# Modulation of the attention layer from plain 32-bit weights in four column groups of TensorE

## Chip, cores, metric

One NeuronCore of a Trainium2 chip runs the whole kernel in one launch. The metric is device time in microseconds (us), the median of several executions. Engines: TensorE (PE, with its weight loads as PEld), VectorE (DVE), ScalarE (ACT), GpSimd (POOL), and SyncE (SP), which issues most of the DMAs.

## What is computed

Two layers over 1024 latent tokens and 256 context tokens of width 1024: windowed attention with a context prefix, then a Conformer convolution module, each with a residual. Only the start matters here, the modulation of the first layer (i = 0):

```python
silu_c = jax.nn.silu(c)            # c: (1, 1024)
silu_cc = jax.nn.silu(c_ctx)       # c_ctx: (1024,)
shift, scale, gate = jnp.split((silu_c @ ada_w[i] + ada_b[i])[:, None, :], 3, axis=-1)
h_lat = modulate(rmsnorm(x, norm_g[i]), shift, scale)          # h * (1 + scale) + shift
shift_c, scale_c, gate_c = jnp.split(silu_cc @ ada_w[i] + ada_b[i], 3, axis=-1)
h_ctx = modulate(rmsnorm(h_ctx_stream, norm_g[i]), shift_c, scale_c)
proj = h_lat @ w_in                # w_in: 1024 x 5120
```

`ada_w[0]` is 1024 x 3072. Two rows, one for the latent and one for the context vector, are multiplied with its first 2048 columns (shift and scale); the gate columns and the second layer's modulation are computed elsewhere and stay as they are.

## The kernel before

The large products are written as three products of a reduced 32-bit type (`F32R`): each operand is rounded to a high part (on ACT) and the rest is kept as a low part (on DVE or POOL), and high x high, high x low and low x high are summed in PSUM (`mm3`). A plain `F32` product is also possible on TensorE and is used in a few places of the kernel, the means of the layer norm among them.

The modulation of layer 1 is worked in four column pairs, `pr` = 0 to 3. A pair covers 256 shift columns and the 256 scale columns that belong to them, which are what two 128-row tiles `kt` of the transposed, modulated input need. For each pair:

- `ada_load(pr)` issues eight 256 KB DMAs on SP into four pages `araw` (each page holds two 128-row slices of the 1024 rows, 512 columns) and two 1 KB DMAs that put the bias into row 4 of a half page `R[pr]`.
- `ada_split(pr)` rounds each page to a high part `ahi` on ACT and subtracts it on DVE to get the low part `alo`.
- `ada_mm(pr)` multiplies on TensorE. The stationary operand is `c4`, 128 rows by 4 columns per slice: high parts of the two silu vectors, then their low parts. The moving operand is a slice of `ahi` or `alo`, 512 columns. Sixteen matmuls, 128*4 by 128x512, accumulate into 4 rows of one PSUM bank. I call these sixteen matmuls a modulation block. DVE copies the four rows to rows 0 to 3 of `R[pr]`.
- `ada_cols(pr)` turns rows into columns: four plain matmuls of `R[pr][0:5]` with a 5 x 2 selection matrix `sel`, which adds high and low rows and the bias. DVE writes the result to `mod`.
- `x_tile(kt)` then modulates a transposed tile of the normalised x: ACT writes the high part `hh`, DVE the full value `hf`, and DVE or POOL the low part `hl`. `c_tile(kt)` does the same for the context.

Around this, `spin(n)` issues matmuls on zeros ahead of the first real work. The loop over `pr` does `ada_mm(pr + 1)`, then 6 or 9 matmuls of `x_mm` for tile 2 pr, the transposes of the next tile of x, `ada_cols(pr + 1)`, `x_mm` of tile 2 pr + 1, and the next transposes. In the third turn two context tiles are worked between. TensorE keeps the program's order in the whole kernel (`PE.on`); DVE keeps it in the opening (`pin("PV")`), ACT only at its very start (`pin("PVA")`); POOL and SP, and later ACT and DVE, are ordered by a planner with a cost model.

The pages `pg` (45 of 4 KB per partition) and half pages `hp` (6) are handed out in the order in which they were freed.

Of the kernel before, what the change touches and what calls it, by code (L numbers as in the profile page):

```python
# [9 lines left out]
F32 = mybir.dt.float32  # L10
F32R = mybir.dt.float32r
AF = mybir.ActivationFunctionType
ALU = mybir.AluOpType

P = 128
# [3 lines left out]
KT = D // P  # L19
# [13 lines left out]
ADA_FP = ()  # L33
# [61 lines left out]
def backbone_kernel(  # L95
# [8 lines left out]
    V, A, G, PE, SY = (InOrder(tc, e) for e in (nc.vector, nc.scalar, nc.gpsimd, nc.tensor, nc.sync))  # L104
# [10 lines left out]
    pg = Pages(pgpool, 45, "page", 1024)  # L115
# [13 lines left out]
    def ps_o(i=None):  # L129
        if i is None:  # L130
            oflip[0] ^= 1
            i = oflip[0]
        return ps.tile([P, 512], F32, tag=f"o{i}", name=nm("pso"), bufs=1)

    def ps_g():
        return ps.tile([P, 512], F32, tag="g", name=nm("psg"), bufs=2)
# [7 lines left out]
    def ctile(shape, dt, name):  # L144
        return cpool.tile(shape, dt, tag=name, name=name, bufs=1)
# [4 lines left out]
    def act(out, in_, func, **kw):  # L150
        return A.activation(out=out, in_=in_, func=func, **kw)

    def tt(eng, out, a, b, op):
        return eng.tensor_tensor(out=out, in0=a, in1=b, op=op)
# [4 lines left out]
    def split_lo(eng, lo, full, hi):  # L159
        return tt(eng, lo, full, hi.bitcast(F32), ALU.subtract)  # L160
# [3 lines left out]
    sel = vt[:, 112:114]  # L164
# [116 lines left out]
    NPR = KT // 2  # L281
    R = {}
    araw = {}

    def ada_load(pr):

        R[pr] = hp.alloc(F32, None, "arow")
        araw[pr] = [pg.alloc(F32, [2, 2, 256], "araw") for _ in range(4)]
        for i in range(4):
            for j in range(2):  # L290
                SY.dma_start(out=araw[pr][i][:, :, j],
                             in_=ada_w[0, i * 256:i * 256 + 256, j * D + pr * 256:j * D + pr * 256 + 256]
                             .rearrange("(k p) n -> p k n", p=P))
        for j in range(2):
            SY.dma_start(out=R[pr][4:5, j * 256:j * 256 + 256], in_=ada_b[0:1, j * D + pr * 256:j * D + pr * 256 + 256])
# [20 lines left out]
    PE.on = True  # L316
    spin(4)
    ada_load(0)
    xs0 = load_rows(x[0, 0:512], 4)
    wsA.load()  # L320
    ada_load(1)
    wsA.load()
    wsA.load()
    ada_load(2)

    cs = ctile([P, 32], F32, "cs")[:, 0:16]
    tp = ps_g()
    PE.transpose(tp[:, 0:32], crow, ident[0:32, 0:32])
    act(cs, tp[:, 0:16], AF.Silu)
# [5 lines left out]
    for t in (pthi, ptlo):  # L335
        for b in (0, 21):
            V.tensor_copy(t[:, b], zer[:, 0:P])
    hp.free(zer_pg)
    c4 = ctile([P, KT, 4], F32R, "c4")
    csv = cs.rearrange("p (r k) -> p k r", r=2)  # L340
    V.tensor_copy(c4[:, :, 0:2], csv)
    tt(V, c4[:, :, 2:4], csv, c4[:, :, 0:2].bitcast(F32), ALU.subtract)

    def sums(ts, engs):

# [23 lines left out]
    Hh, Hl = [], []  # L369
    Hc = []  # L370

    cf = ctile([P, KT, 4], F32, "cf")
    G.memset(cf[:, :, 2:4], 0.0)
    V.tensor_copy(cf[:, :, 0:2], csv)

    def modulated(psrc, dsts, s, b, n, lo_eng, twice=False):

        f = pg.alloc(F32, [1024], "hf")
        if twice is True:
            act(dsts[0][0], psrc, AF.Identity, scale=s, bias=b)  # L380
        if twice == "A":
            act(f[:, 0:n], psrc, AF.Identity, scale=s, bias=b)
        else:
            V.tensor_scalar(out=f[:, 0:n], in0=psrc, scalar1=s, scalar2=b, op0=ALU.mult, op1=ALU.add)
        for dh, dl, view in dsts:
            if twice is not True:
                act(dh, view(f), AF.Copy)
            split_lo(lo_eng, dl, view(f), dh)
        pg.free(f)

    def ada_split(pr, which=range(4)):
        for i in which:
            if (pr, i) not in ADA_FP:
                raw = araw[pr][i]
                rv = raw.rearrange("p a b c -> p a (b c)")
                h, l = pg.alloc(F32R, [2, 512], "ahi"), pg.alloc(F32R, [2, 512], "alo")
                act(h, rv, AF.Copy)
                split_lo(V, l, rv, h)
                pg.free(raw)
                araw[pr][i] = (h, l)  # L400

    def ada_mm(pr):

        o = ps_o(0)
        for i in range(4):
            for k in range(2):
                if (pr, i) in ADA_FP:
                    r = araw[pr][i].rearrange("p a b c -> p a (b c)")
                    parts = [(cf, r)]
                else:  # L410
                    parts = [(c4, r) for r in araw[pr][i]]
                for n, (c, r) in enumerate(parts):
                    PE.matmul(o[0:4], c[:, 2 * i + k, :], r[:, k], start=i + k + n == 0,
                              stop=i + k == 4 and n == len(parts) - 1)
            pg.free(*(araw[pr][i] if len(parts) == 2 else (araw[pr][i],)))
        V.tensor_copy(R[pr][0:4, 0:512], o[0:4])

    def ada_cols(pr):

        rw, m = R.pop(pr), mods[pr]  # L420
        cps = ps_o(1)
        for i in range(4):
            PE.matmul(cps[:, 2 * i:2 * i + 2], rw[0:5, i * P:(i + 1) * P], sel[0:5], start=True, stop=True)
        hp.free(rw)
        with tc.high_priority():
            V.tensor_copy(m[:, 0:2], cps[:, 0:4].rearrange("p (a b) -> p a b", b=2))
            for i in range(2):
                V.tensor_scalar(out=m[:, 2 + i], in0=cps[:, 4 + 2 * i:6 + 2 * i], scalar1=1.0,
                                scalar2=vt[:, 96 + 2 * pr + i:97 + 2 * pr + i], op0=ALU.add, op1=ALU.mult)
# [58 lines left out]

    pin("PVA")
    ada_split(0)  # L490
    spin(10)
    ss0 = sums(xs0, (A, A, A, A))
    ada_mm(0)
    ada_cols(0)
    spin(18)
    r0 = rstd_of(ss0, D, 4)
# [11 lines left out]
    x_mm(1, 0, acc0, (0,))  # L508
    pin("PV")
    ada_split(1)  # L510
    wsA.split()
    wsA.split()
    for pr in range(NPR):
        a, b = 2 * pr, 2 * pr + 1
        which = range(3) if pr else (1, 2)
        if pr + 1 < NPR:
            ada_mm(pr + 1)
        if pr + 2 < NPR:
            ada_split(pr + 2, (0, 1))
# [3 lines left out]
        if pr + 1 < NPR:  # L523
            tp = turn(xs0, a + 2, ps_g)
            ada_cols(pr + 1)
            x_tile(tp, a + 2, 0, V)
        else:
            turn_vecs(*vec_pages)
            x_tile(turn(xs1, 0, ps_g), 0, 1, V)
# [600 lines left out]
    for i, (h, qb) in enumerate(steps):  # L1130
# [26 lines left out]
        if regroup:  # L1157
            g = nxt[0] // 4
# [545 lines left out]
def _constants():  # L1704
    f = np.float32
    grid_w, base, half = 64, 10000.0, HD // 2
    n_axis = HD // 4
    t = np.arange(T)
    row, col = (t // grid_w).astype(f), (t % grid_w).astype(f)
    inv = np.power(f(base), -np.arange(n_axis, dtype=f) / f(n_axis)).astype(f)  # L1710
    ang = np.concatenate([row[:, None] * inv, col[:, None] * inv], axis=-1).astype(f)
    cos, sin = np.cos(ang).T.astype(f), np.sin(ang).T.astype(f)
    k_cos = np.concatenate([cos, cos], 0)
    k_sin = np.concatenate([-sin, sin], 0)
    i, j = np.arange(P)[:, None], np.arange(P)[None, :]
    z = np.zeros((P, P), f)
    prev = np.where(j >= i, f(0), f(NEG)).astype(f)
    nxt = np.where(j <= i, f(0), f(NEG)).astype(f)
    k_mask = np.concatenate([prev, z, nxt, z, z], 1)
    sel = np.zeros((P, 2), f)  # L1720
    sel[[0, 2, 4], 0] = 1
    sel[[1, 3, 4], 1] = 1
    return {"k_cos": k_cos, "k_sin": k_sin, "k_mask": k_mask, "k_ident": np.eye(P, dtype=f), "k_sel": sel}


# [22 lines left out]
```

## Time and profile before

| | |
|---|---|
| median of 3 runs | 1731.13 us (1729.16 to 1732.06) |
| the profiled execution's own time | 1733.08 us |
| its span, first to last instruction | 1731.3 us |
| mean granted TensorE clock | 0.995 |
| PE busy | 98% of the span |
| DVE, ACT, POOL busy | 64%, 51%, 52% |
| DMA | 242.45 MB, 140 GB/s on average |

In a line of the profile, L89 is a helper through which nearly all instructions pass, so instructions are told apart by tile names: `out<-in`, then partitions x elements, type and count. In a timeline the first two numbers are start and duration in us, and square brackets hold the idle time before the instruction and what ended it. Matmul durations are modelled and overlap: the distance from start to start tells what one costs in a stream.

### The profile page before, as it was taken

The page shows a single profiled execution, that of the slowest core. Times are in us where ns is not written, and L with a number is a line of the kernel's source. Part 1 is how long each engine was busy: PE and PEld are TensorE (multiplying, and loading weights), DVE is VectorE, ACT ScalarE, POOL GpSimd, SP SyncE. Part 2 cuts the span into 40 slices and gives each one's busy share as a digit, 9 for nine tenths or more (in the row PEclk, how much of TensorE's full clock was granted, in tenths as well). Part 3 has the DMA queues.
Part 4 walks back from the last instruction along what each step waited for, and adds up shares of the span by engine and source line. Part 5 has one row for each costly group of instructions (what it writes and reads, how often), then busy time and mean ns, then how long its engine had stood idle before and what let it go on. Part 6 is the DMA issues. An engine that isn't in the chain of part 4 may idle for free.

```text
span 1731.3 us, 23940 instructions
## 1 busy us (share of the span) xinstructions
PE 1699.9 (98%) x8420; PEld 1427.4 (82%) x8420; DVE 1109.0 (64%) x2095; ACT 889.3 (51%) x1548; POOL 896.0 (52%) x741
## 2 busy tenths in 40 slices
PE   8999999999999999999999999999999999999997
PEld 4788888888888888888888888888888888787886
DVE  6655553555445553556315279999999999867823
ACT  7555553555445453545333355564665564466731
POOL 0255654566636565553101257999998888130300
PEclk9999999999999999999999999999999999999999
DMA  9234443444334442436777723011121302377971
GB/s 341 78 89 141 136 137 80 149 149 147 101 107 145 148 147 78 150 110 203 258 260 243 264 86 110 25 49 37 41 82 37 92 31 80 122 250 252 321 276 49
DMA packets 195324, 242.45 MB, mean 140 GB/s; under 512 B 11798, under 2 KB 126790, under 8 KB 195204
## 3 DMA queue, kind: packets, MB, share of 16 engines
q1 hardware_dynamic: 188516, 230.10, 40.1%
q10 hardware_dynamic: 6688, 10.83, 2.5%
q8 instruction: 66, 1.08, 0.3%
q14 instruction: 54, 0.44, 0.1%
HBM read 188.70 MB, written 41.69 MB: 133 GB/s over the span
## 4 chain that ended last, share of the span: by engine, by line
PE 89%; DMA 4%; DVE 3%; ACT 1%; POOL 1%; issue 1%; SPq 1%; ACTq 0%; DVEq 0%; POOLq 0%
PE psg L89 46%; PE pss L89 23%; PE pso L89 20%; DMA low_page<-in_conv_w_out_dram 1%; DMA rope_half<-rope_half 1%; DMA araw_page<-in_ada_w_dram 1%; DVE alo_page L89 1%; SPq L89 1%; DMA wo_page<-in_conv_w_out_dram 0%; POOL rope_half L89 0%; DVE hf_page L89 0%; POOL low_page L89 0%; ACT hh_page L89 0%; DMA ozf_page<-ozd 0%; ACT lhi_half L89 0%
## 5 line engine op out<-in xcount | busy, mean ns | idle before, releaser
L89 POOL TENSOR_TENSOR odd_half<-odd_half,prod_half 128x513 f32<-128x513 f32 (+2 forms) x252 | 314.2, 1254 | 23.0 <-ACT prod_half L89 9.8
L89 PE MATMUL psg<-hh_page,whi_page 128*128 128x512 f32 x600 | 236.2, 394 | 0.0
L89 PE MATMUL psg<-hl_page,whi_page 128*128 128x512 f32 x600 | 235.1, 392 | 0.0
L89 PE MATMUL psg<-hh_page,wlo_page 128*128 128x512 f32 x600 | 234.4, 391 | 0.0
L89 ACT ACTIVATE prod_half<-ubuf,dww 128x513 f32<-128x513 f32 (+2 forms) x252 | 165.6, 675 | 115.9 <-POOL odd_half L89 111.9
L89 POOL TENSOR_TENSOR wlo_page<-wraw_page,whi_page 128x512 fp32r<-128x512 f32 (+1 forms) x106 | 177.6, 1692 | 89.3 <-ACT whi_page L89 61.5
L89 POOL TENSOR_SCALAR p_page<-p_page,sc 128x640 f32<-128x640 f32 (+1 forms) x128 | 99.3, 776 | 224.3 <-DVE sc L89 212.8
L89 PE MATMUL psg<-h2h_page,whi_page 128*128 128x512 f32 x464 | 182.0, 392 | 0.0
L89 PE MATMUL psg<-h2h_page,wlo_page 128*128 128x512 f32 x464 | 180.8, 390 | 0.0
L89 PE MATMUL psg<-h2l_page,whi_page 128*128 128x512 f32 x464 | 180.7, 389 | 0.0
L89 DVE SCALAR_TENSOR_TENSOR pss<-ubuf,dww,pss 128x512 f32<-128x512 f32 (+3 forms) x270 | 172.7, 672 | 0.1
L89 DVE SCALAR_TENSOR_TENSOR pss<-ubuf,wsum,pss 128x512 f32<-128x512 f32 (+3 forms) x270 | 172.0, 672 | 0.2
L89 DVE TENSOR_TENSOR ptlo<-pss,pthi 128x640 fp32r<-128x640 f32 (+1 forms) x144 | 103.5, 719 | 84.9 <-ACT pthi L89 83.7
L89 ACT ACTIVATE p_page<-p_page,sc 128x641 f32<-128x641 f32 (+1 forms) x128 | 102.6, 802 | 77.8 <-DVE sc L89 73.6
L89 ACT ACTIVATE pthi<-pss 128x640 fp32r<-128x640 f32 (+1 forms) x144 | 88.7, 616 | 102.8 <-PE pss L89 96.4
L89 PEld LDWEIGHTS psg<-hh_page,wlo_page 128*128 128x128 f32 x600 | 113.0, 188 | 24.6
L89 PEld LDWEIGHTS psg<-hh_page,whi_page 128*128 128x128 f32 x600 | 113.1, 188 | 19.4
L89 PEld LDWEIGHTS psg<-hl_page,whi_page 128*128 128x128 f32 x600 | 113.2, 189 | 18.5
L89 ACT ACTIVATE whi_page<-wraw_page 128x1024 fp32r<-128x1024 f32 x88 | 92.5, 1052 | 57.9 <-PE psg L89 20.3
L89 PE MATMUL pso<-h2l_page,whi_page 128*128 128x512 f32 x304 | 118.4, 389 | 0.0
L89 PE MATMUL pso<-h2h_page,whi_page 128*128 128x512 f32 x304 | 118.4, 389 | 0.0
L89 PE MATMUL pso<-h2h_page,wlo_page 128*128 128x512 f32 x304 | 118.3, 389 | 0.0
(244 smaller groups left out, 4063.4 us busy)
## 6 DMA issues: line engine op xcount, KB each, us to landing
wraw_page<-in_conv_w_in_dram SPq DMA_DIRECT2D x48, 512.0 KB
wraw_page<-in_attn_w_in_dram SPq DMA_DIRECT2D x40, 512.0 KB
wol_page<-wolA SPq DMA_DIRECT2D x32, 512.0 KB
wo_page<-in_attn_w_out_dram SPq DMA_DIRECT2D x32, 512.0 KB
wo_page<-in_conv_w_out_dram SPq DMA_DIRECT2D x32, 512.0 KB
wol_page<-wolC SPq DMA_DIRECT2D x32, 512.0 KB
rope_half<-rope_half ACTq DMA_DIRECT2D x80, 128.0 KB
araw_page<-in_ada_w_dram SPq DMA_DIRECT2D x32, 256.0 KB
```

Of the source, the lines that this page charges most:

```text
L89: r = f(*a, **k)
```

## The change

The weights are no longer split. `ada_mm` multiplies the `araw` pages as they come from DMA, as plain `F32`, with a stationary operand `c32` of 32 columns per slice: the two silu vectors, then 30 columns of zeros. Eight products make a block. They are dealt to the four column groups of TensorE (`tile_position=(0, g)`, `g` = 0, 32, 64, 96, two products each), and each group writes its own 32 rows of the PSUM bank. `R[pr]` is filled with zeros on POOL ahead of the bias DMA; DVE adds the whole bank to it in place of the copy of four rows. `ada_cols` now sums over all 128 rows, and `sel` is 1 at rows g and g + 2 for the first column, g + 1 and g + 3 for the second, and 1 at row 4 (the bias) for both. The small tiles `c4` and `cf` go; `cs` is declared wider by as much, so other tiles keep their place. `c32` takes a page.

```diff
     def ada_load(pr):
 
         R[pr] = hp.alloc(F32, None, "arow")
+        G.memset(R[pr][:, 0:512], 0.0)
         araw[pr] = [pg.alloc(F32, [2, 2, 256], "araw") for _ in range(4)]
...
-    cs = ctile([P, 32], F32, "cs")[:, 0:16]
+    cs = ctile([P, 96], F32, "cs")[:, 0:16]
...
+    c32 = pg.alloc(F32, [KT, 32], "c32")
+    csv = cs.rearrange("p (r k) -> p k r", r=2)
+    G.memset(c32, 0.0)
+    V.tensor_copy(c32[:, :, 0:2], csv)
     hp.free(zer_pg)
-    c4 = ctile([P, KT, 4], F32R, "c4")
-    csv = cs.rearrange("p (r k) -> p k r", r=2)
-    V.tensor_copy(c4[:, :, 0:2], csv)
-    tt(V, c4[:, :, 2:4], csv, c4[:, :, 0:2].bitcast(F32), ALU.subtract)
...
-    cf = ctile([P, KT, 4], F32, "cf")
-    G.memset(cf[:, :, 2:4], 0.0)
-    V.tensor_copy(cf[:, :, 0:2], csv)
...
     def ada_split(pr, which=range(4)):
-        for i in which:
-            if (pr, i) not in ADA_FP:
-                raw = araw[pr][i]
-                rv = raw.rearrange("p a b c -> p a (b c)")
-                h, l = pg.alloc(F32R, [2, 512], "ahi"), pg.alloc(F32R, [2, 512], "alo")
-                act(h, rv, AF.Copy)
-                split_lo(V, l, rv, h)
-                pg.free(raw)
-                araw[pr][i] = (h, l)
+        pass
 
     def ada_mm(pr):
 
         o = ps_o(0)
         for i in range(4):
+            rv = araw[pr][i].rearrange("p a b c -> p a (b c)")
             for k in range(2):
-                if (pr, i) in ADA_FP:
-                    r = araw[pr][i].rearrange("p a b c -> p a (b c)")
-                    parts = [(cf, r)]
-                else:
-                    parts = [(c4, r) for r in araw[pr][i]]
-                for n, (c, r) in enumerate(parts):
-                    PE.matmul(o[0:4], c[:, 2 * i + k, :], r[:, k], start=i + k + n == 0,
-                              stop=i + k == 4 and n == len(parts) - 1)
-            pg.free(*(araw[pr][i] if len(parts) == 2 else (araw[pr][i],)))
-        V.tensor_copy(R[pr][0:4, 0:512], o[0:4])
+                g = 64 * (i % 2) + 32 * k
+                PE.matmul(o[g:g + 32], c32[:, 2 * i + k, :], rv[:, k], start=i < 2, stop=i > 1,
+                          tile_position=(0, g))
+            pg.free(araw[pr][i])
+        if pr == NPR - 1:
+            pg.free(c32)
+        r = R[pr][:, 0:512]
+        tt(V, r, o, r, ALU.add)
 
     def ada_cols(pr):
...
-            PE.matmul(cps[:, 2 * i:2 * i + 2], rw[0:5, i * P:(i + 1) * P], sel[0:5], start=True, stop=True)
+            PE.matmul(cps[:, 2 * i:2 * i + 2], rw[:, i * P:(i + 1) * P], sel, start=True, stop=True)
...
     sel = np.zeros((P, 2), f)
-    sel[[0, 2, 4], 0] = 1
-    sel[[1, 3, 4], 1] = 1
+    for g in range(0, P, 32):
+        sel[[g, g + 2], 0] = 1
+        sel[[g + 1, g + 3], 1] = 1
+    sel[4] = 1
```

## The prediction

> **What bounds the kernel now.** I read the page first, then busy time and clock by stretch, then TensorE's timeline between 20 and 62 us, where the changed code runs.
>
> ```profile
> PE 1699.9 (98%) x8420; PEld 1427.4 (82%) x8420; DVE 1109.0 (64%) x2095; ACT 889.3 (51%) x1548; POOL 896.0 (52%) x741
> ```
>
> ```profile
> 0.00:24.00 24.00, 18.74 (x68) 11.97 (x69) 10.98 (x26) 17.31 (x23) 0.92 (x7) 0.93 0.89 301
> 24.00:62.00 38.00, 34.41 (x158) 20.78 (x157) 31.95 (x52) 27.40 (x39) 7.01 (x6) 0.96 0.69 250
> 100.00:800.00 700.00, 695.23 (x3867) 606.05 (x3866) 356.00 (x797) 339.82 (x726) 399.07 (x361) 1.00 0.41 128
> ```
>
> The columns are busy time on PE, PEld, DVE, ACT and POOL, then granted clock, DMA share and GB/s. From 100 us on TensorE hardly waits: 4.8 us in 700. It keeps its program order throughout, so the opening matters only through the moment at which it hands over. The change touches nothing behind about 60 us; whatever TensorE is early or late there is carried to the end. So I walk along TensorE's opening. These rows are its timeline: the first product of a modulation block, or the first matmul behind one.
>
> ```profile
> 28.06 0.39 PE L89 MATMUL pso<-ahi_page,c 128*4 128x512 f32 x1
> 32.72 0.39 PE L89 MATMUL pss<-hh_page,whi_page 128*128 128x512 f32 x1
> ...
> 37.99 0.48 PE L89 MATMUL pso<-ahi_page,c 128*4 128x512 f32 x1
> 42.76 0.40 PE L89 MATMUL pss<-hh_page,whi_page 128*128 128x512 f32 x1
> ...
> 44.84 0.60 PE L89 MATMUL psg<-ident,x_page 128*128 128x128 f32 x4
> 45.37 1.05 PE L89 MATMUL pso<-vt,arow_half 5*128 5x2 f32 x8
> 46.35 0.50 PE L89 MATMUL pss<-hh_page,whi_page 128*128 128x512 f32 x1
> ...
> 48.53 0.60 PE L89 MATMUL psg<-ident,x_page 128*128 128x128 f32 x4
> 48.89 0.48 PE L89 MATMUL pso<-ahi_page,c 128*4 128x512 f32 x1
> 52.83 0.39 PE L89 MATMUL pss<-hh_page,whi_page 128*128 128x512 f32 x1
> ...
> 54.90 0.60 PE L89 MATMUL psg<-ident,x_page 128*128 128x128 f32 x4
> 55.43 1.05 PE L89 MATMUL pso<-vt,arow_half 5*128 5x2 f32 x8
> 56.41 0.44 PE L89 MATMUL pso<-ident,x_page 128*128 128x128 f32 x2
> 57.72 0.54 PE L89 MATMUL pso<-ident,x_page 128*128 128x128 f32 x2 [0.87 <-DVE mod L89]
> 57.91 0.78 PE L89 MATMUL pss<-hh_page,whi_page 128*128 128x512 f32 x1
> ...
> 61.62 0.60 PE L89 MATMUL psg<-ident,x_page 128*128 128x128 f32 x4
> ```
>
> With the four blocks numbered 0 to 3, blocks 1 to 3 are shown. They last 4.66, 4.77 and 3.94 us, together 13.37. Nine matmuls of 512 columns take 52.83 to 54.90, or 0.230 each; sixteen make 3.68, so 2.3 us of the 13.37 is waiting. The stretches between blocks are 5.27, 6.13 and, up to 57.91, 5.08 us.
>
> **The change, part by part.** Splits removed: sixteen roundings on ACT and sixteen subtractions on DVE.
>
> ```profile
> L89 DVE TENSOR_TENSOR alo_page<-araw_page,ahi_page 128x1024 fp32r<-128x1024 f32 x16 | 19.3, 1243 | 4.2 <-ACT ahi_page L89 4.1
> L89 ACT ACTIVATE ahi_page<-araw_page 128x1024 fp32r<-128x1024 f32 x16 | 16.3, 1051 | 4.3 <-DMA araw_page<-in_ada_w_dram 4.3
> ```
>
> 19.3 us of DVE and 16.3 us of ACT go. That is not the gain: only what TensorE waits for counts.
>
> Block 0 runs ahead of anything that needs it. What TensorE needs next are the scaled rows of x; ACT's sums over them waited for the rows to arrive (first line below):
>
> ```profile
> 14.46 1.06 ACT L89 ACTIVATE junk_page<-x_page 128x1024 f32<-128x1024 f32 x1 [0.28 <-DMA x_page<-in_x_dram]
> 19.66 2.20 ACT L89 ACTIVATE x_page<-x_page,r 128x1024 f32<-128x1024 f32 x2
> 21.76 1.99 ACT L89 ACTIVATE ahi_page<-araw_page 128x1024 fp32r<-128x1024 f32 x2
> 22.52 1.03 PE L89 MATMUL psg<-ident,x_page 128*128 128x128 f32 x8
> 23.65 1.42 ACT L89 ACTIVATE hh_page<-psg,mod 128x512 fp32r<-128x512 f32 x2
> 26.74 0.69 DVE L89 TENSOR_TENSOR hl_page<-hf_page,hh_page 128x512 fp32r<-128x512 f32 x1
> ```
>
> So rows are ready at 21.86 as before and I book nothing up to there; the transposes can start then, not at 22.52. But two weight roundings sat on ACT between 21.76 and 23.65, ahead of the first modulated tile. Without them it starts near 22.7, and the chain ending in the last row (27.43) ends near 26.5. Block 1 starts at 27.1 instead of 28.06: gain 0.95.
>
> A block now has eight plain products instead of sixteen. Their price is the unknown. The nearest rows are the plain products of the later layer norm, of full width (one of them in the timeline, then the group of four instructions):
>
> ```profile
> 1480.72 1.10 PE L89 MATMUL pso<-vsum_page,ones 128*128 128x512 f32 x2 [1.61 <-DVE vsum_page L89]
> L89 PE MATMUL pso<-vsum_page,ones x4: 592/592/668, 1480.7 to 1560.1; 128*128 128x512 f32 x4
> ```
>
> One plain product is two instructions of 0.592 each. A matmul here lasts 0.39 at a pitch of 0.23, so 0.16 of it is a tail that the next one covers; a half then costs 0.592 - 0.16 = 0.43, and 0.47 with its start-up, (1.10 - 0.16) / 2, where it stands alone. I take 0.43, as a block is a stream. Bounds for eight: one after another, 16 x 0.43 = 6.88; all four groups at once, two rounds of two halves, 1.72. No row has two column groups, so the trace excludes neither. I take a value between, for a reason: TensorE's starts follow program order, and the second half of a product needs the same column group as its first half. It can't start before the first ends, but the next product, in another group, can start beside it. Each product then overlaps the next by one half: nine steps, 3.87. For entering and leaving the grouped mode I charge the tail of 0.16 twice. A block is 4.2, three are 12.6, against 13.37: gain 0.75. No subtraction is waited for any more; the arrays come straight from DMA:
>
> ```profile
> 32.61 3.90 ACT L89 ACTIVATE ahi_page<-araw_page 128x1024 fp32r<-128x1024 f32 x4 [1.75 <-DMA araw_page<-in_ada_w_dram]
> 40.31 1.06 ACT L89 ACTIVATE junk_page<-x_page 128x1024 f32<-128x1024 f32 x1 [0.23 <-DMA x_page<-in_ctx_dram]
> ```
>
> Block 2's four arrays were there between 32.6 and about 35.4, block 3's before the context rows issued behind them, so before 40.3. In the walk below both are in time.
>
> The Trainium skill ("TensorE: Matmul & The Clock Gate", Part 3) reports 2.38x for three column tiles at 512 columns, and matmuls that start and end strictly in order. By its ratio eight products take about 2.9 us, an estimate, and three blocks about 3 us less than in my sum; no run here shows it. Against the change stands "TensorEngine Tiling (Array Packing)" of the Trainium skill, Key Properties: a change of tiling mode drains the engine; no run here shows what that costs.
>
> Between blocks the same work stays: matmuls at 0.230, transposes, eight tiny column matmuls. Those now load 128 rows instead of 5:
>
> ```profile
> 1508.90 0.95 PE L89 MATMUL pso<-ones,qa_half 128*128 128x1 f32 x8
> L89 DVE COPY arow_half<-pso 4x512 f32<-4x512 f32 x4 | 2.7, 675 | 1.2 <-PE pso L89 1.2
> L89 DVE TENSOR_TENSOR rope_page<-pss,cos_page 128x512 f32<-128x512 f32 x2 | 1.4, 688 | 0.9 <-ACT rope_half L89 0.9
> 0.87 0.53 POOL L89 MEMSET zer_half<- 128x512 f32 x1
> L89 SPq DMA_DIRECT2D arow_half<-in_ada_b_dram x8: 246/250/322, 6.9 to 34.2; - x8
> ```
>
> Eight with 128 rows take 0.95, eight with 5 rows 1.05: nothing. The bias add in place of the copy: 688 against 675 ns, nothing. Four POOL fills of 0.53 and a smaller one precede the bias DMAs, so SP's queue waits on POOL there, with the weight loads behind it; POOL is done near 4 us, the first bias DMA (last row) goes at 6.9, hence free. If POOL were late, all loads behind would slip with it.
>
> Without waits the first stretch is 12 matmuls (2.76), two sets of transposes (0.53 and 0.36) and the columns (0.98), 4.6 in place of 5.27. The second is 18 matmuls and the same, 6.0 in place of 6.13. The third holds 0.87 of waiting for the modulation, which DVE delivered late; its copy and two small operations stay, so I count 0.75. Together 1.5, as DVE no longer has subtractions queued ahead.
>
> The last term is the clock:
>
> ```profile
> 58.00:60.00 2.00, 2.00 (x7) 1.61 (x6) 0.50 (x1) 1.97 (x5) 2.00 (x3) 0.50 0.04 8
> 60.00:62.00 2.00, 2.00 (x9) 1.58 (x9) 1.81 (x4) 0.37 (x1) 0.64 (x1) 0.68 0.00 0
> ```
>
> After 54.90 to 57.91, 3.0 us without a wide matmul, the granted clock was 0.50 and nine matmuls took 57.91 to 61.62, 1.64 more than their 2.07. The gap shrinks to 2.3; the one from 44.84 to 46.35 (1.5) had no such effect, as 46.35 to 48.53, nine matmuls at 0.24, shows. I take it that the clock stays: 1.64, at even odds.
>
> **Sum:** 0.95 + 0.75 + 1.5 = 3.2, with the clock 4.84. The profiled execution took 1733.08 (span 1731.3 and 1.8 around it), 1.95 above the median of the three runs; from the median, 1731.13 - 4.84 = 1726.3, or 1727.9 without the clock's part.
>
> **Rivals.** *The products run one after another (slower).* Block 6.88 + 0.32 = 7.2, three 21.6: 8.2 more than before. The other terms give back 2.45, or 4.1 with the clock, so 4.1 to 5.8 later: 1735 to 1737. It decides once a block exceeds (13.37 + 4.1) / 3 = 5.8. For it: the two halves of the plain product above don't overlap, 1.10 for both. Against: they use the same columns.
>
> *All four groups run at once.* A block is 1.72 + 0.32 = 2.04. The second of the three then waits for its arrays, to about 36.5; the third ends near 44.6, and the stretch behind it would be over by 48.9. But the modulation copy stands on DVE behind the row statistics of the second half of x, whose last sum ended here:
>
> ```profile
> 50.80 0.18 ACT L89 ACTIVATION_READ_ACCUMULATOR junk_page<-x_page 128x1 f32 x1
> ```
>
> Two roundings of 1.05 stood before it on ACT, so it moves to near 49; with an estimated 2 us of small operations and the copy, 51.3 instead of 57.91, gain 6.6, or 8.2 with the clock: 1723 to 1724.5. The ratio that the Trainium skill gives for three tiles ("TensorE: Matmul & The Clock Gate", Part 3), above, lies between this case and mine.
>
> *The gain is lost elsewhere.* ACT, POOL and SP are ordered by a planner; earlier freed engines may put a load or a sum badly and TensorE waits behind 62 us. Price: the 4.84 are gone, 1731; if as much again is lost, 1736. Against it: 4.8 us of waiting in 700.
>
> **How the numbers follow.** Pairwise overlap 0.40, one after another 0.30, all at once 0.24, lost elsewhere 0.06. About 0.2%, 3.5 us, is what a measurement can tell from no change. Of the pairwise case 0.28 lies beyond it and 0.02 turns out slower; of all at once 0.22 lies beyond; one after another gives 0.29 slower, the last rival 0.06. Faster 0.50, same 0.13, slower 0.37. The range takes all at once and reaches into one after another: 1723 to 1736.5; the likeliest case alone is 1724.5 to 1728.5.
>
> **What would show it.** Grouped products of a block: the first half of a product starting together with the second half of the one before it means pairwise; 0.43 behind that, serial; together with the first half of the one before, all at once. Block lengths 4.2, 7.2 or 2.0. Block 1 starting at 27.1. Wide matmuls behind block 3 starting near 54.5 with clock 1.00. The prediction is wrong if blocks exceed 5.8, if TensorE waits for arrays, or if the handover at 100 us doesn't move as 57.91 does.

## The result: 4.5 us faster, by another way than forecast

The changed kernel takes 1726.16 us (median of 8 runs, 1723.83 to 1728.95); the kernel before took 1730.68 beside it (8 runs, 1727.42 to 1732.06). The ratio is 0.9977, 95% interval 0.9966 to 0.9988; by it the gain is 4.0 us, between 2.1 and 5.9, and by the medians 4.5. The forecast was 1726.3. The profiled execution took 1728.0 us, 5.1 under the 1733.08 of before; its span is 1726.2.

The page's busy times first, then busy time and clock by stretch (PE, PEld, DVE, ACT, POOL, granted clock, DMA share, GB/s):

```profile
PE 1692.5 (98%) x8420; PEld 1423.5 (82%) x8420; DVE 1090.0 (63%) x2077; ACT 873.8 (51%) x1532; POOL 899.1 (52%) x745
```

```profile
0.00:24.00 24.00, 17.24 (x68) 10.27 (x69) 7.40 (x21) 12.29 (x18) 3.55 (x11) 0.97 0.87 297
24.00:62.00 38.00, 33.22 (x183) 23.22 (x182) 21.08 (x47) 19.68 (x35) 8.31 (x7) 0.88 0.72 254
100.00:800.00 700.00, 694.98 (x3865) 605.29 (x3864) 356.78 (x798) 337.29 (x720) 398.92 (x361) 1.00 0.41 128
```

DVE lost 19.0 us and ACT 15.5, close to the 19.3 and 16.3 of the groups of before. Between 100 and 800 us TensorE waits 5.0 us in 700, as against 4.8 before. Between 24 and 62 us the mean clock fell from 0.96 to 0.88, which the forecast did not have. TensorE's timeline shows why (start, duration; in brackets the wait and what ended it):

```profile
27.15 1.92 PE L89 MATMUL pso<-araw_page,c_page 128*32 128x512 f32 x16
...
33.77 1.92 PE L89 MATMUL pso<-araw_page,c_page 128*32 128x512 f32 x16
...
41.73 1.93 PE L89 MATMUL pso<-araw_page,c_page 128*32 128x512 f32 x16
43.59 0.50 PE L89 MATMUL pss<-hh_page,whi_page 128*128 128x512 f32 x1
...
46.84 1.05 PE L89 MATMUL pso<-vt,arow_half 128*128 128x2 f32 x8 [0.46 <-DVE arow_half L89]
47.75 0.42 PE L89 MATMUL pso<-ident,x_page 128*128 128x128 f32 x2
51.84 0.66 PE L89 MATMUL pso<-ident,x_page 128*128 128x128 f32 x2 [3.67 <-DVE mod L89]
52.16 0.78 PE L89 MATMUL pss<-hh_page,whi_page 128*128 128x512 f32 x1
...
56.14 0.90 PE L89 MATMUL psg<-ident,x_page 128*128 128x128 f32 x4
```

A block lasts 1.85 to 1.86 us (27.15 to the next wide matmul at 29.01; 33.77 to 35.62; 41.73 to 43.59) where it lasted 4.66, 4.77 and 3.94. By the end of block 3 TensorE is 9.24 us ahead (52.83 less 43.59). Then it stands for 3.67 us, before the transposes of the second context tile. They need the PSUM bank from which DVE has yet to read the modulation, and DVE (its timeline, in program order) was held by something else:

```profile
46.09 0.69 DVE L89 TENSOR_TENSOR arow_half<-pso,arow_half 128x512 f32<-128x512 f32 x1
49.95 0.17 DVE L89 TENSOR_SCALAR ms<-ssx 128x4 f32<-128x4 f32 x1 [3.17 <-ACT junk_page L89]
...
51.21 0.16 DVE L89 TENSOR_TENSOR r<-rr,rq 128x4 f32<-128x4 f32 x1
51.29 0.15 DVE L89 COPY mod<-pso 128x4 f32<-128x4 f32 x1
```

```profile
49.73 0.19 ACT L89 ACTIVATION_READ_ACCUMULATOR junk_page<-x_page 128x1 f32 x1
```

The copy of the modulation stands behind six small operations on the statistics of the second half of x, and the first of those waits for ACT's last sum, at 49.92. The column sums on TensorE had been done at 47.9. Of the lead 5.75 is left when tile 5 (the sixth of the eight 128-row tiles of the modulated input) starts at 52.16. And it starts cold, that is at half clock, as the same stretch by 2 us shows:

```profile
48.00:50.00 2.00, 0.17 (x2) 0.00 (x0) 0.05 (x1) 2.00 (x6) 0.00 (x0) 0.98 0.99 332
50.00:52.00 2.00, 0.16 (x1) 0.19 (x2) 1.29 (x9) 0.96 (x3) 0.47 (x1) 0.50 0.52 205
52.00:54.00 2.00, 2.00 (x6) 1.63 (x6) 0.74 (x1) 1.97 (x4) 2.00 (x3) 0.50 0.04 8
54.00:56.00 2.00, 2.00 (x6) 1.55 (x5) 1.97 (x4) 0.12 (x1) 0.84 (x1) 0.50 0.00 0
```

Nine matmuls take 52.16 to 56.14, 3.98 us, against about 2.1 at full clock. The clock fell at 49.92, 1.75 us into the wait, and came back at 56.75. The lead is then 5.48 (61.62 less 56.14) and 5.08 at the end.

### The profile page after: what moved, and what is told of

It reads as the page before. It is cut to its first block, busy times and chain, and to the rows that moved or that the text cites. A ratio compares the mean times of both kernels' runs of the same rounds, so it can differ in the third digit from the quotient of the medians.

```text
span 1726.2 us, 23896 instructions
## 1 busy us (share of the span) xinstructions
PE 1692.5 (98%) x8420; PEld 1423.5 (82%) x8420; DVE 1090.0 (63%) x2077; ACT 873.8 (51%) x1532; POOL 899.1 (52%) x745
## 4 chain that ended last, share of the span: by engine, by line
PE 91%; DMA 3%; ACT 2%; DVE 2%; POOL 1%; issue 1%; SPq 0%; ACTq 0%; DVEq 0%; POOLq 0%
PE psg L89 47%; PE pss L89 24%; PE pso L89 20%; DMA low_page<-in_conv_w_out_dram 1%; DMA rope_half<-rope_half 1%; POOL rope_half L89 0%; DMA wo_page<-in_conv_w_out_dram 0%; DMA x_page<-in_x_dram 0%; DMA araw_page<-in_ada_w_dram 0%; SPq L89 0%; ACT junk_page L89 0%; ACT hh_page L89 0%; ACT lhi_half L89 0%; ACT x_page L89 0%; POOL wlo_page L89 0%
```

## Experiments

Each is an edit of the changed kernel unless it says of before. "Tile 5" and "tile 7" are the `x_mm` matmuls of these tiles; in the changed kernel they start at 52.16 and 61.47, before at 57.91 and 66.59. Where I say "matched", I compare the start of the same TensorE instruction, counted from the end of the program, in the profiled executions of two kernels.

### What a plain product costs, and which of them overlap

**plain_one_array**: the kernel before, all products plain on the undivided array, by a switch that it already has.

```diff
-ADA_FP = ()
+ADA_FP = tuple((p, i) for p in range(4) for i in range(4))
```

> The kernel before with all its weight slices taken by its own plain 32-bit path: no split, eight plain products in a block, no column groups, four columns of weights. Theory A (block length counts, and the changed kernel gains by running four groups at once): 16 halves of 0.43 make a block of 6.9 us, three of them 15 us longer than in the changed kernel; the 3.7 us wait for the modulation copy and the half clock behind it (1.9) should go, so 9.5 to 11.5 us slower than the changed kernel, 1736 to 1738. Theory B (only the freed DVE and ACT count): like the changed kernel, 1726.

**one_group**: the changed kernel with every product in group 0.

```diff
-PE.matmul(o[g:g + 32], ..., start=i < 2, stop=i > 1, tile_position=(0, g))
+PE.matmul(o[0:32], ..., start=i + k == 0, stop=i + k == 4, tile_position=(0, 0))
-tt(V, r, o, r, ALU.add)
+tt(V, r[0:32], o[0:32], r[0:32], ALU.add)
```

> The changed kernel with all eight products of a block in column group 0. Theory A: nothing overlaps, block 6.9 to 7.1 us, time as with the plain path of the kernel before, 1736 to 1738; a difference between the two would be the price of the grouped mode, at most 0.2 us a block by the changed kernel's trace. Theory B: 1726.

**two_groups**: `g = 32 * k`, four products in each of two groups, the bias added on 64 rows.

> The changed kernel with the products dealt to two column groups instead of four. Theory A: block 3.5 to 3.7 us if two run at once, 4.1 if the second half of a product holds back the next product (the prediction's pairwise overlap). Three blocks are then 5 us longer than with four groups, but 3.7 of that falls into the wait for the modulation copy, so the time should be nearly that of the changed kernel: 1726 to 1728. If no such wait caps the gain, 1731.

**by_page**: `g = 32 * i`, so that the two products of one group follow each other directly.

> The changed kernel with both products of a page in the same column group (groups 0, 0, 32, 32, 64, 64, 96, 96 in program order) instead of neighbours in different groups. If every group has a queue of its own, the block stays at 1.9 us and the time at 1726. If a product that waits for its group holds back those behind it, products overlap only where the group changes: 13 steps of 0.43, block 5.6 us, and the time falls between two groups and one group, 1728 to 1732.

Block 1 and the first matmul behind it, from the four timelines of TensorE, in this order:

```profile
27.35 7.03 PE L89 MATMUL pso<-araw_page,cf 128*4 128x512 f32 x16
34.31 0.50 PE L89 MATMUL pss<-hh_page,whi_page 128*128 128x512 f32 x1
```

```profile
27.89 7.05 PE L89 MATMUL pso<-araw_page,c_page 128*32 128x512 f32 x16
34.88 0.50 PE L89 MATMUL pss<-hh_page,whi_page 128*128 128x512 f32 x1
```

```profile
26.80 3.63 PE L89 MATMUL pso<-araw_page,c_page 128*32 128x512 f32 x16
30.36 0.50 PE L89 MATMUL pss<-hh_page,whi_page 128*128 128x512 f32 x1
```

```profile
27.15 1.94 PE L89 MATMUL pso<-araw_page,c_page 128*32 128x512 f32 x16
29.02 0.50 PE L89 MATMUL pss<-hh_page,whi_page 128*128 128x512 f32 x1
```

| | block 1, us | time, us | ratio to before |
|---|---|---|---|
| undivided array | 6.96 | 1737.39 | 1.0038 (1.0024 to 1.0052) |
| one group | 6.99 | 1735.09 | 1.0023 (1.0011 to 1.0035) |
| two groups | 3.56 | 1723.80 | 0.9959 (0.9944 to 0.9973) |
| four groups, by page | 1.87 | 1726.40 | 0.9967 (0.9954 to 0.9979) |
| four groups, as changed | 1.86 | 1726.16 | 0.9977 (0.9966 to 0.9988) |

The kernel before, run beside them, took 1730.57 for the first three rows, 1732.23 for by_page and 1730.68 for the last, so the ratios compare better than the times. Sixteen halves in 6.96 us are 0.435 each, the 0.43 of the forecast. The grouped mode with one group adds 0.03 to a block; four groups take 1.86 where four halves in a row make 1.74, so entering and leaving cost at most 0.12.

Two groups divide the block by 1.96, four by 3.76: groups run beside each other, and a half waits only for the half before it in its own group. Pairwise overlap would have given 4.2 with two groups as with four, and by_page, where a product's neighbour in the order is in its own group, would have taken 5.6. Both are excluded. The starts within by_page's block say it directly: they come in fours, at 27.15 to 27.19, 27.60 to 27.64, 28.03 to 28.07 and 28.46 to 28.50. In program order the first four halves all belong to group 0, and halves of one group start 0.43 apart (one_group), so the four that start together are of four groups: starts don't follow the program's order across groups.

The first two rows are the rival "one after another", which was put at 1735 to 1737, 4.1 to 5.8 later than before: by their ratios the runs are 4.0 and 6.6 later, one just short of that span and one beyond it.

The time does not follow the block. From one group to two, 3.43 us less per block bring 11.3 us in all; from two to four, another 1.70 per block bring nothing. two_groups is even ahead, where 1726 to 1728 was expected: 1723.80 and, in a second run beside the changed kernel,

> The kernel with two column groups once more, beside the one with four in the same call. If its lead is real: 2 to 3 us under it, about 1723.8. If it was the chance of one call: 1726, no difference.

> The changed kernel as it is, for comparison on the same chip: 1726, 0.9975 of the kernel before.

1724.91 (1721.99 to 1727.55, 6 runs) against 1726.36 (1725.34 to 1729.71, 6 runs), ratios to before 0.9959 (0.9944 to 0.9973) and 0.9971 (0.9957 to 0.9984). The intervals overlap, so the lead of 1.5 to 2.4 us is likely and not settled; matched at 100 us, two_groups is 1.4 ahead and, in the second pair, 0.7. With two groups TensorE arrives 4 us later at the place of the wait, and finds no long one and a clock that stays:

```profile
52.50 0.41 PE L89 MATMUL pso<-ident,x_page 128*128 128x128 f32 x2 [0.33 <-DVE mod L89]
```

```profile
50.00:52.00 2.00, 2.00 (x17) 1.76 (x16) 1.20 (x7) 0.84 (x3) 0.64 (x2) 1.00 0.95 371
52.00:54.00 2.00, 1.67 (x10) 1.31 (x9) 0.41 (x4) 2.00 (x4) 2.00 (x3) 1.00 0.07 18
```

Tile 5 starts at 52.66, 0.5 behind the changed kernel, and tile 6 is 1.6 ahead of it.

### Are short blocks enough by themselves?

**splits_kept**: the roundings and subtractions put back, with results that nobody reads.

```diff
     def ada_split(pr, which=range(4)):
-        pass
+        for i in which:
+            rv = araw[pr][i].rearrange("p a b c -> p a (b c)")
+            h, l = pg.alloc(F32R, [2, 512], "ahi"), pg.alloc(F32R, [2, 512], "alo")
+            act(h, rv, AF.Copy)
+            split_lo(V, l, rv, h)
+            pg.free(h, l)
```

> The changed kernel with the sixteen roundings on ACT and subtractions on DVE put back where the kernel before has them; their results are not used, TensorE still multiplies the unsplit weights in four groups. Theory A (both are needed: DVE's queue of subtractions sets when modulated tiles are ready, so short blocks alone only make TensorE wait): near the kernel before, 1729 to 1732. Theory B (short blocks alone bring the gain): near the changed kernel, 1726.

1735.19 (10 runs) beside 1732.23 for the kernel before, ratio 1.0010 (1.0001 to 1.0020): the gain is gone. TensorE's waits between 20 and 100 us (total, times, longest):

```profile
PE pso L89 <- DVE arow_half L89: 3.9, 2, 3.0
PE pss L89 <- DVE hl_page L89: 3.1, 4, 1.1
PE psg L89 <- DVE x_page L89: 1.8, 2, 1.5
PE pss L89 <- DVE wlo_page L89: 1.4, 2, 1.3
```

In the changed kernel the first two are 0.5 and 0.6. The sum that TensorE waited 3.0 us for stood on DVE behind two subtractions (52.10 to 54.45) and the first statistics. None of TensorE's waits in these 80 us is for a load. So neither part pays alone: without the splits, but with 7 us blocks, the ratios to before are 1.0023 and 1.0038; with blocks of 1.9 to 2.5 us, but the splits, 1.0010. What the freed DVE bought is that it delivers in time for a TensorE that comes earlier.

### Can the wait be moved?

**stats_later** (changed kernel) and **before_stats_later** (kernel before): the statistics behind the modulation in DVE's order.

```diff
-        if pr == 2:
-            normalise(xs1, ss1, (G, G, A, G))
         x_mm(a, 0, acc0, which)
         if pr + 1 < NPR:
             tp = turn(xs0, a + 2, ps_g)
             ada_cols(pr + 1)
             x_tile(tp, a + 2, 0, V)
+            if pr == 2:
+                normalise(xs1, ss1, (G, G, A, G))
```

> The changed kernel with the row statistics and scaling of the second half of x written behind the last modulation copy and the tile that uses it, in place of ahead of it; nothing else. Theory A (the copy waits on DVE behind those statistics): the 3.7 us wait of TensorE goes, the next nine matmuls start near 48.7 instead of 52.2 and at full clock, 5.4 us earlier there; some is lost again as the scaled rows come later, so 1721 to 1724. Rival (the rows of x themselves come too late, and any order waits for them): 1726, with the wait moved to the transposes of the second half.

> The kernel before with the row statistics of the second half of x written behind the last modulation copy, nothing else. If the wait that caps the changed kernel were there already before, this alone gains what it gains there. By the trace of before the copy waited 0.87 us and not on the statistics' input, so at most 0.9 us plus the half clock of 1.6: 1728 to 1731; if the scaled rows then come too late, as in the changed kernel with the same edit, up to 1733.

**stats_fast**: the same move, the statistics with priority in the planner, the first and the last of the four row tiles scaled on DVE.

```diff
+                with tc.high_priority():
+                    normalise(xs1, ss1, (V, G, A, V))
```

> The changed kernel with the statistics of the second half of x behind the last modulation copy, put ahead by the planner where they are ready, and its four row tiles scaled by DVE, POOL, ACT, DVE instead of POOL, POOL, ACT, POOL. With the statistics merely moved, TensorE waited 3.3 us for rows that POOL scaled one after another (4.0 us for three) and ACT's square root came 2.5 us late. If that is all that took the gain back, the wait goes and the time is 1720 to 1723; if the rows still come late because ACT's sums end near 50 us, 1725 to 1727.

None of them gains on the kernel that it edits, and stats_later and stats_fast are slower than either of their theories had put them. stats_later 1728.76 (11 runs, 0.9986, 0.9976 to 0.9997), stats_fast 1728.41 (10 runs, 0.9980, 0.9969 to 0.9991), before_stats_later 1733.71 (10 runs, 1.0014, 1.0003 to 1.0024). In the changed kernel the long wait goes, and tile 5 starts at 49.49 and at 48.71. But the scaled rows of the second half come later, and TensorE waits for them or for DVE behind them. The waits of stats_later, then of stats_fast:

```profile
PE psg L89 <- POOL x_page L89: 3.3, 3, 1.7
...
PE pso L89 <- DVE mod L89: 0.3, 1, 0.3
```

```profile
PE pso L89 <- DVE abt L89: 3.1, 1, 3.1
PE psg L89 <- DVE x_page L89: 2.2, 3, 1.2
...
PE pso L89 <- DVE mod L89: 0.3, 1, 0.3
```

Tile 7 starts at 61.73 and 60.90, against 61.47. The rows of the second half are summed on ACT until about 50, and what hangs on them has to pass DVE, POOL and ACT; put behind the modulation, it is late for TensorE in its place. And the half clock comes with the new waits. In stats_later it covers most of tile 5 and all of tile 7:

```profile
50.00:52.00 2.00, 2.00 (x6) 1.55 (x5) 0.69 (x1) 2.00 (x6) 0.00 (x0) 0.50 0.98 380
...
62.00:64.00 2.00, 2.00 (x6) 1.59 (x5) 1.89 (x4) 1.56 (x5) 0.00 (x0) 0.50 0.00 0
```

In stats_fast tile 7 takes 3.99 us (60.90 to 64.89) instead of 2.16. Matched at 100 us, the two are 3.2 and 1.5 behind the changed kernel. In stats_later the clock fell at 49.06 although the waits about there were only 1.3 and 0.3 us long; column sums and transposes ran between them, and the last wide matmuls had ended near 46.

In the kernel before the move only costs: its wait for `mod` was 0.87 us long, so there was little to gain.

### What does the wait itself cost, and what the clock?

**filled**: fifteen matmuls without use, into a PSUM bank that is free then, just ahead of the waiting transposes. The wait for DVE stays.

```diff
             c_tile(ctodo.popleft(), 0)
+            if pr == 2:
+                for _ in range(15):
+                    PE.matmul(acc0[3], wsA.hl[0][0][:, 0], Hh[0][:, 0:512], start=True, stop=True)
             c_tile(ctodo.popleft(), 1)
```

> The changed kernel with fifteen matmuls of 128x512 whose result nobody reads, put on TensorE between the two context tiles of the third turn, where it otherwise waits 3.67 us for the modulation. The wait itself stays. Theory 1 (the half clock after the wait costs what it seems to): x_mm of tile 5 starts at 52.2 as before but at full clock, nine matmuls in 2.1 instead of 3.98 us, and at least 1.5 us of that is still there at 80 us: about 1724.5. Theory 2 (the rows of the second half of x bound what follows, as where the statistics were moved): tile 5 is faster by 1.9, but tile 7 starts near 61 as in the changed kernel and the time is 1726, no difference.

**cover**: the matmuls of tile 5 in that place instead.

```diff
         if pr > 1:
             c_tile(ctodo.popleft(), 0)
+        if pr == 2:
+            x_mm(b, 0, acc0, which)
+        if pr > 1:
             c_tile(ctodo.popleft(), 1)
-        x_mm(b, 0, acc0, which)
+        if pr != 2:
+            x_mm(b, 0, acc0, which)
```

> The changed kernel with the nine matmuls of x_mm of tile 5 in the third turn put ahead of the second context tile, whose transposes have to wait until DVE has read the modulation out of their PSUM bank. The matmuls then stand under the wait, at full clock. Theory 1 (wait and clock both cost): tile 5 from 48.3 to 50.4, the context tile's transposes at about 51.8, tile 6 some 3 to 4 us earlier, the time 1723 to 1724. Theory 2 (the rows of the second half bound): tile 7 not before 60.9, the time 1725.5 to 1726.5.

filled is the best kernel of the study: 1722.35 (1719.85 to 1723.55, 5 runs), ratio to before 0.9942 (0.9927 to 0.9956), just below the interval of the changed kernel beside it (0.9957 to 0.9984). Its timeline and its clock at the place:

```profile
48.30 3.68 PE L89 MATMUL pss<-hh_page,whi_page 128*128 128x512 f32 x15
52.21 0.41 PE L89 MATMUL pso<-ident,x_page 128*128 128x128 f32 x2 [0.23 <-DVE mod L89]
52.38 0.48 PE L89 MATMUL pss<-hh_page,whi_page 128*128 128x512 f32 x1
...
54.54 0.60 PE L89 MATMUL psg<-ident,x_page 128*128 128x128 f32 x4
```

```profile
52.00:54.00 2.00, 1.79 (x9) 1.56 (x10) 0.44 (x2) 2.00 (x3) 2.00 (x2) 1.00 0.04 14
```

Tile 5 starts where it did and takes 2.16 instead of 3.98 us. Tile 7 starts at 59.84, 1.63 earlier, although block 1 had begun 0.40 later. That is theory 1, and the rows of the second half do not take it back.

The medians differ by 4.0 us, more than this term. Matched with the changed kernel, filled is 1.7 us ahead at 100 us, 1.5 at 570 and 6.6 at the end: the filling itself brought about 1.7, and the rest arose further on, mostly about two waits that the edit does not touch. Here they are in the timeline of the changed kernel, and then the first of them in filled:

```profile
577.44 0.45 PE L89 MATMUL pss<-kh_page,qh_page 128*128 128x384 f32 x1 [3.17 <-DVE ptlo L89]
```

```profile
812.92 0.59 PE L89 MATMUL pso<-mask_page,ones 128*1 128x256 f32 x2 [1.70 <-DVE mask_page L89]
```

```profile
574.48 0.44 PE L89 MATMUL pss<-kh_page,qh_page 128*128 128x384 f32 x1 [1.73 <-DVE ptlo L89]
```

The clock behind them differs between executions, of one and the same kernel too. The stretches around them in the changed kernel, in its second run (after_again; the first of the waits is this row), and in filled:

```profile
577.91 0.44 PE L89 MATMUL pss<-kh_page,qh_page 128*128 128x384 f32 x1 [3.09 <-DVE ptlo L89]
```

```profile
560.00:600.00 40.00, 36.83 (x201) 32.14 (x201) 19.55 (x46) 17.07 (x38) 22.96 (x22) 0.96 0.47 145
800.00:840.00 40.00, 38.30 (x206) 32.86 (x205) 22.03 (x41) 25.18 (x42) 8.98 (x12) 0.96 0.81 279
```

```profile
560.00:600.00 40.00, 36.91 (x210) 32.44 (x209) 20.00 (x48) 18.67 (x43) 23.83 (x22) 1.00 0.50 156
800.00:840.00 40.00, 38.23 (x210) 32.77 (x209) 22.23 (x41) 24.31 (x41) 8.64 (x11) 1.00 0.82 292
```

```profile
560.00:600.00 40.00, 38.27 (x220) 33.78 (x219) 20.39 (x48) 20.40 (x45) 22.09 (x21) 1.00 0.52 162
800.00:840.00 40.00, 37.88 (x205) 32.03 (x204) 20.28 (x37) 23.45 (x36) 7.24 (x17) 1.00 0.83 292
```

0.96 over 40 us is about 1.6 us lost, twice. Matched, after_again is 0.5 us behind the first run at 570 us and 2.2 ahead at 820: one and the same kernel varies by some 3 us here, without a difference in its work. Whether the shorter wait in filled is chance as well is not shown. All five of its runs lie below all six of the changed kernel beside it, so that it is faster is clear; how much of the 4.0 beyond 1.7 is due to the edit stays open.

cover took 1725.98 (1722.80 to 1727.92, 8 runs), ratio to before 0.9962 (0.9949 to 0.9976): no difference from the changed kernel that can be told. Tile 5 runs under the wait, 47.74 to 49.9. TensorE then waits 1.62 for `mod`, 0.82 for ACT to read a context tile and 1.02 for the low part of tile 6, and its clock halves a little later, 0.51 between 56 and 58 us. Tile 7 starts at 59.91, before the 60.9 that theory 2 had set as the earliest. So useful work under the wait gained no more at that point than useless work: what it saved was waited for behind it. Matched at 100 us, cover is 1.3 ahead of the changed kernel, against the 1.7 of filled.

## Why the prediction was right, step by step

The time was right, the sum was not, and that they agree is luck. What happened in the blocks is the rival "All four groups run at once", given 0.24, by the sign that the prediction had set for it: first halves start together, at 27.15 to 27.17. The terms of the sum, as the gain of TensorE over the kernel before in the two profiled executions:

| step | predicted, us | measured, us |
|---|---|---|
| start of block 1 | 0.95 | 0.91 (28.06 to 27.15) |
| blocks 1 to 3 | 0.75 | 7.80 (13.37 to 5.57) |
| two stretches between blocks | 0.75 | 0.53 (4.76 and 6.11 us long) |
| third stretch, to tile 5 | 0.75 | -3.49 (5.08 to 8.57) |
| nine matmuls of tile 5 | 1.64 | -0.27 (3.71 to 3.98) |
| sum there | 4.84 | 5.48 |
| at the end | 4.84 | 5.08 |

**Up to block 1.** Right: without the two weight roundings ACT started the first modulated tile at 22.64 (forecast 22.7), and the chain ended on DVE at 26.43 (26.5). That block 1 itself came within 0.04 is chance: in the second run of the same kernel it started at 26.75.

**A half of a plain product, 0.43.** Right: 0.435 in the run on the undivided array. The way of getting it, duration of a lone instruction less the tail read from a stream, held.

**Pairwise overlap.** Wrong, and the term that was mis-sized most: 4.2 us a block predicted, 1.86 measured. The step that failed is its premise, "TensorE's starts follow program order": a second half does wait for the first half in its group, but the products behind it are not held back. The starts in by_page show it, and two_groups gives 3.56. The rival "all four groups at once" had 2.04. The Trainium skill ("TensorE: Matmul & The Clock Gate", Part 3) gives 2.38x for three column tiles; four gave 3.76x here and two 1.96x, with plain 32-bit operands, so its direction was the better guide. That matmuls start strictly in order, which the prediction took from the same part, does not hold across column groups here. The charge of 0.32 for the grouped mode was too high as well: one group measures 0.03 over the undivided array, and four groups at most 0.12 over four halves in a row. The drain at a change of mode that "TensorEngine Tiling (Array Packing)" names in its Key Properties can cost no more than these 0.03 to 0.12 us at this place.

**The third stretch.** Wrong, and this is what brought the time back. The step "its copy and two small operations stay, so I count 0.75" took the delivery of the modulation to move with TensorE. It does not once a block is short: it is tied to ACT's last sum. The limit stood in the all-at-once rival, with 51.3 for tile 5; 52.16 was measured, since the last sum moved from 50.98 to 49.92 and not to 49.

**The clock.** Wrong, as one of two even odds: the wide matmuls behind block 3 were to start near 54.5 at clock 1.00, and started at 52.16 at 0.50, behind a wait of 3.67 us. In the sum above it cost nothing against before, where tile 5 was cold too. filled shows what it was worth: 1.8 us on those nine matmuls, 1.6 of it still there at tile 7. The idea that the gap would shrink to 2.3 us fell with the third stretch. The Trainium skill ("TensorE: Matmul & The Clock Gate", Part 1) says that the gate goes by a free-running window of about 3.4 us, so that the phase decides. The traces agree: the wait of 3.67 us halved the clock in both runs of the changed kernel and in by_page, but 1.8, 2.9 and 0.8 us after it had begun, and every stretch at half clock between 20 and 100 us, in all the runs, lasts 3.4 or 6.8 us. A later wait lasted 3.2 and 3.1 us in the two runs of the changed kernel and cost 0.04 of the clock around it in one and nothing in the other.

**Behind.** Right: 5.75 ahead at the start of tile 5 and 5.48 at its end are 5.3 at 100 us (matched) and 5.08 at the end. "Lost elsewhere" did not happen; the bias add (0.69 us) and the column sums over 128 rows (0.95 and 1.05) cost nothing, and no load was late.

So the forecast came out because two errors of 7 and about 6 us were against each other. Without the new wait (3.67) and the half clock (1.9) the lead of 5.48 behind tile 5 would have been about 11 us, an estimate; the reorderings tried (stats_later, stats_fast, cover) did not get at them, as each time a later wait, and half clock with it, came in their place.

## What to carry to other kernels

Small products that share no rows of their output can be dealt to column groups of TensorE, also in plain 32-bit: each group runs on its own, and dropping the split of the operands frees DVE and ACT, which is where the gain is cashed. When a stretch becomes much shorter, look for what the next consumer waits for in another engine's program order before counting the gain: here 7.8 us of shorter blocks gave 3.5 back at one copy. Where such a wait can't be removed, filling it with matmuls that keep the clock up can pay: about 1.7 us here, where shortening the blocks from two groups to four brought nothing. Measure it several times, since a wait of about 3 us costs half clock in some executions and not in others.

## What the runs showed of the hardware

- Plain 32-bit matmuls of 32 stationary columns and 512 moving columns: sixteen halves in 6.99 us in one column group, 3.56 in two, 1.86 in four. The order in which groups are issued makes no difference (1.86 and 1.87): halves of different groups start together though the program has those of one group next to each other.
- Sixteen halves in one column group take 0.03 us more than on the undivided array (6.99 and 6.96).
- Fifteen dummy matmuls in a wait of 3.67 us kept the clock at 1.00; without them it was 0.50 for 6.8 us.
- Between 20 and 100 us the clock stays at half for 3.4 or 6.8 us in every run in which it falls. The same wait of 3.67 us was followed by the fall 0.8, 1.8 and 2.9 us after its start in three executions.
